# Feature-major input tiles for layer 0, with row factors taken through memory, on one Trainium2 core

## The chip, the cores and the metric

The kernel runs on one core of one Trainium2 chip. The metric is the device time of one execution in microseconds (us). The kernel before was run three times: 3614.48, 3615.36 and 3619.56 us, with a median of 3615.36 us. A separate profiled execution gives the profile and the trace.

The engines are TensorE (PE, with its weight loads shown as PEld), VectorE (DVE), ScalarE (ACT), GpSimd (POOL) and SyncE (SP), which here only issues DMA transfers. ACT and POOL issue transfers too.

## The reference, cut to what matters

The reference is a two-layer backbone over 2304 rows: 256 context rows and 2048 latent rows, 1024 features each. Layer 0 (even) runs latent attention and bidirectional gated linear attention side by side; layer 1 (odd) runs neighbourhood attention. The change touches only how layer 0 makes its normalised and modulated input h, which is the first thing that layer computes:

```
h = rms_norm(x, norm_g[i]) * (1 + scale) + shift      # scale, shift from the conditioning vector
u = h @ w_in                                          # 1056 latent columns first: 768 q, 256 kv, 32 rope
q = rms_norm(q_lat) @ w_uq ; kv = rms_norm(kv_lat) @ w_ukv ; q, k = rms_norm per head, then rope
```

`rms_norm` divides each row by the root of the mean of its squares. So each row of x has one factor, and each feature has one scale and one shift. All arithmetic is in float32. Matmul operands are split in a high and a low part, and each product is three matmuls (high x high, high x low, low x high).

## The kernel before, in words

**Tiles.** The 2304 rows are 18 tiles of 128 rows (`NT`); tiles 0 and 1 are context. A matmul contracts over the partitions, so h must lie with features on the partitions: 8 groups of 128 features (`KD`), each 128 features x 128 rows.

**The stage.** `even_latent` (called once, at the start of the program) holds layer 0's latent projections, up to about 540 us of the span. Tiles 0 and 1 are prepared ahead of its loop. The loop of L584 runs `s` from 0 to 19, and step `s` writes this work:

- `prep(0, s+1)`: makes the input of the next tile. `transposed` (L322) loads 128 rows of `xin` with rows on the partitions (L326, 512 KB, SP), ACT squares them with a running sum for each row (L106, into the tile `hlo`, as a scratch), POOL makes the factor by a power of -1/2 (`rpow`, L204 and L206), DVE scales the rows (L332), and PE transposes the eight 128x128 blocks into the PSUM tiles `px` (L335). `modulate` (L338) then has ACT take each block out of PSUM with the feature's scale and shift (eight instructions, all under L106, the line of the helper `act`), DVE makes the high part (L347, `hhi`) and the low part (L348, `hlo`), and ACT issues the store of h to memory for later stages (L349, `H`).
- `gemm(s)`: three chunks of 352 latent columns, each 24 matmuls of 352 (L120 to L122, PSUM tile `gm`), copied by ACT to `u`, then squares and factors for the latents' norms (`scaled`; DVE scales at L471 and L472).
- `ada`: one or two steps of the conditioning rows for later use. Eight loads of weights (L277, `adaw`, 256 KB each, two buffers), for each two DVE instructions (L280, L282), then two matmuls and a few small instructions (L287 to L311, among them the ones that make `modA` and `modB`, L304 and L306).
- `up(s-1)`: PE transposes the latents (L499, `tp`), ACT and DVE make their high and low parts (`lth`, and `ltl` at L502), 36 matmuls of 384 columns for q and 12 of 512 for k and v (`up`), then norms for each head on ACT, DVE and POOL (L520 to L541).
- `fin(s-2)`: PE transposes q and k for each head (L554), ACT and DVE make high and low parts (`qkhl`, L561), SP stores them (L563). The last tile's keys go through the PSUM tile `px`. In the last steps `first` computes chunks of the next stage for the last two tiles (again `gm` matmuls, now with `W0` to `W2` of that stage).

**What sets the order.** Each engine runs its instructions in the order of its own queue. This order is not the written one: a scheduler that builds the program arranges the instructions of the loop's steps across each other, within the dependences, the number of buffers, and `issue_after`, by which an instruction comes no sooner in the order than another. The conditioning steps are bound to come after the load of x (`self.xload`) in this way. Buffers matter here: `x` has one, `hhi` and `hlo` two each, `adaw` two, `wraw` (raw weights on their way to high and low parts) two, `px`, `tp`, `gm` and `up` two in PSUM.

Of the kernel before, what the change touches and what calls it, by code (L numbers as in the profile page):

```python
# [10 lines left out]
F32 = mybir.dt.float32  # L11
F32R = mybir.dt.float32r
AF = mybir.ActivationFunctionType
ALU = mybir.AluOpType
# [3 lines left out]
P = 128  # L18
D = 1024
KD = D // P  # L20
# [3 lines left out]
NT = T // P  # L24
NCT = CTX // P
EPS = 1e-6
# [19 lines left out]
def win_start(ax, q):  # L46
    n, w, _ = AXES[ax]
    return min(max(q - w // 2, 0), n - w)
# [40 lines left out]
class Kern:  # L89
# [248 lines left out]
    def modulate(self, l, t, x, ps, hi, lo):  # L338
# [10 lines left out]
        nc.scalar.dma_start(self.H[l, t], x[:])  # L349
        return hi, lo  # L350

    def reload(self, l, t):

        nc, sp = self.nc, self.prp
        x = self.tl(sp, [P, D], "x", bufs=1)
        nc.sync.dma_start(x[:], self.H[l, t])
        h = x[:].rearrange("p (k t) -> p k t", k=KD)
        hi = self.tl(sp, [P, KD, P], "hhi", F32R, bufs=self.hbufs)
        lo = self.tl(sp, [P, KD, P], "hlo", F32R, bufs=self.hbufs)
        self.act(hi[:], h)  # L360
        nc.vector.tensor_tensor(out=lo[:], in0=h, in1=hi[:], op=ALU.subtract)
        return hi, lo
# [34 lines left out]
    def even_latent(self, ws, wrest, kept):  # L397
        nc, tc = self.nc, self.tc
        self.QT = self.scr("QT", (A_HEADS, 2, A_QK + 1, T), F32)
        self.KT = self.scr("KT", (A_HEADS, 2, A_QK + 1, T), F32)  # L400
        self.Vn = self.scr("Vn", (P, NT, 512), F32)
        self.Un = self.scr("Un", (NT, P, 1568), F32)
        with ExitStack() as es:
            pp = self.pool(es, "epA", bufs=2, space=PSUM, reuse_waits="tile")
            px = ("px", 2)
            hT, lat, nat, win = {}, {}, {}, {}
            with ExitStack() as es2:
# [4 lines left out]
                hi, lo = win[0] = [self.tl(ws, [P, KD, LAT_CHUNK], "W0" + z, F32R, bufs=1) for z in "hl"]  # L412
# [8 lines left out]
            sp = self.pool(es, "esA", bufs=2, side="left", reuse_waits="tile")  # L421
# [21 lines left out]
            def gemm(*ts):  # L443
                us = {}
                for j in range(3):
                    for t in ts:
                        hi, lo = hT[t]
                        ps = self.tl(pp, [P, LAT_CHUNK], "gm", bufs=2)
                        wh, wl = win[j]
                        self.mm3(ps[:], (lambda k: hi[:, k, :], lambda k: lo[:, k, :]),  # L450
                                 (lambda k: wh[:, k, :], lambda k: wl[:, k, :]), range(KD))
                        if j == 0:
                            us[t] = self.tl(sp, [P, LAT_COLS], "u", bufs=2)
                        self.act(us[t][:, j * LAT_CHUNK : (j + 1) * LAT_CHUNK], ps[:])
                for t in ts:
                    parts = hT.pop(t)
                    if t >= NT - self.hbufs:
                        kept[t] = parts
                    scaled(t, us[t])
# [124 lines left out]
            for s in range(NT + 2):  # L584
                if 0 < s < NT - 1:
                    with tc.issue_after(behind.ins) if s == 1 else ExitStack():
                        hT[s + 1] = self.prep(0, s + 1, self.i["xin"], pp, px)
                if s == 0:
                    gemm(0, 1)
                elif 1 < s < NT:  # L590
                    gemm(s)
                for _ in range((s > 1) + (s in (6, 10))):
                    with tc.issue_after(self.xload.ins):
                        next(ada, None)
                for f, d in ((up, 1), (fin, 2)):
                    if s >= NT - 1:
                        for _ in zip(range(3), ahead):
                            pass
                        if f == fin and s >= NT:
                            first(NT - 1, s - NT + 2)  # L600
                            first(NT - 2, s - NT + 2)
                    if 0 <= s - d < NT:
                        f(s - d)
# [1197 lines left out]
def layout(I):  # L1801

    f = lambda a: np.ascontiguousarray(a, dtype=np.float32)
    o = {}
    o["xin"] = f(np.concatenate([I["ctx"][0], I["x"][0]], 0))
    o["cond"] = f(np.stack([I["c"][0], I["c_ctx"]], -1).reshape(KD, P, 2).transpose(1, 0, 2))
    o["norm_g"] = f(I["norm_g"].reshape(2, KD, P).transpose(2, 0, 1))
    o["ada_w"] = f(I["ada_w"].reshape(2, KD, P, 6, 512).transpose(0, 2, 3, 1, 4))
    o["ada_bc"] = f(I["ada_b"][0, : 2 * D].reshape(2, KD, P).transpose(2, 0, 1))
    o["ada_b"] = f(np.broadcast_to(I["ada_b"][:, None, :], (2, 2, 3 * D)))  # L1810
    w = I["ev_w_in"][0].reshape(KD, P, -1).transpose(1, 0, 2)
    o["w_lat"] = f(w[:, :, :LAT_COLS].reshape(P, KD, 3, LAT_CHUNK).transpose(0, 2, 1, 3))
    o["w_uq"] = f(I["ev_w_uq"][0].reshape(6, P, 768).transpose(1, 0, 2))
    o["w_ukv"] = f(I["ev_w_ukv"][0].reshape(2, P, 1024).transpose(1, 0, 2))
    o["lat_norm"] = f(np.concatenate([I["ev_q_norm"][0].reshape(6, P).T, I["ev_kv_norm"][0].reshape(2, P).T], 1))
    qkg = np.ones((P, 4), np.float32)
    row = np.zeros((2, 32), np.float32)
    for z, g in enumerate((I["ev_q_gain"][0], I["ev_k_gain"][0])):
        qkg[:96, 2 * z] = g
        qkg[:64, 2 * z + 1] = g[:64]  # L1820
        row[z] = g[64:]
    o["qk_gain_col"] = qkg
    o["qk_gain_row"] = row.reshape(1, 2, 32)
    t = np.arange(SEQ)
    inv = np.float32(10000.0) ** (-np.arange(0, 16, 2, dtype=np.float32) / np.float32(16))
    ang = np.stack([(t // 64).astype(np.float32)[:, None] * inv, (t % 64).astype(np.float32)[:, None] * inv], 1)
    cos, sin = np.cos(ang), np.sin(ang)
    C = np.stack([cos, cos], 2).reshape(16, P, 32).transpose(1, 0, 2)
    S = np.stack([-sin, sin], 2).reshape(16, P, 32).transpose(1, 0, 2)
    o["rope_cos"], o["rope_sin"] = f(C), f(S)  # L1830
    r = w[:, :, LAT_COLS:]
    parts = [r[:, :, :512], r[:, :, 1568:], r[:, :, 512:864], r[:, :, 864:1216], r[:, :, 1216:1568]]
    o["w_rest"] = f(np.concatenate([a.reshape(P, -1) for a in parts], 1))
    gw = np.zeros((97, 2, 256), np.float32)
    for z in range(2):
        for r in range(z * 16, 96, 32):
            gw[r : r + 16, z] = I["ev_gate_w"][0, z]
        gw[96, z] = I["ev_gate_b"][0, z]
    o["gate_w"] = f(gw.reshape(97, 2, 4, 64).transpose(0, 2, 1, 3).reshape(97, 512))
    m, l = np.arange(P)[:, None], np.arange(P)[None, :]  # L1840
    tri = np.stack([(m <= l) * 1.0 - (m <= 63), (m >= l) * 1.0 - (m >= 64), m <= l, m >= l], 1)
    o["tri"] = f(tri)
    o["halves"] = f(np.stack([np.arange(P) < 64, np.arange(P) >= 64], 1))
    o["gla_norm"] = f(I["ev_gla_norm"][0].reshape(4, P).T)
    o["w_out0"] = f(I["ev_w_out"][0].reshape(KD, P, D).transpose(1, 0, 2))
    o["w_od"] = f(I["od_w_in"][0].reshape(KD, P, 8, 512).transpose(1, 2, 0, 3))
    o["od_gain"] = f(np.stack([np.tile(I["od_q_gain"][0], 2), np.tile(I["od_k_gain"][0], 2)], 1))
    o["w_out1"] = f(I["od_w_out"][0].reshape(KD, P, D).transpose(1, 0, 2))
    rpb = I["od_rpb"][0]
    for kind in "kq":  # L1850
        off, bad = [], []
        for ax, (_, w, u) in enumerate(AXES):
            start = lambda p: np.array([win_start(ax, x) for x in p.ravel()]).reshape(p.shape)
            at = np.array([p for _, p in BLOCKS[kind][ax]])[None, :]
            own = np.array([g * u for g, _ in BLOCKS[kind][ax]])[None, :] + np.arange(u)[:, None]
            k, q = (own, at) if kind == "k" else (at, own)
            off.append(np.clip(k - q + w - 1, 0, 2 * w - 2))
            bad.append(np.where((k >= start(q)) & (k < start(q) + w), 0, -1e30) * np.ones(off[ax].shape))
        tab = rpb[:, off[0]][..., off[1]]
        if kind == "k":  # L1860
            o["rpb_k"] = f(tab.transpose(0, 3, 1, 2, 4).reshape(16, P, -1))
            rows, cols = np.tile(bad[0], (16, 1)), np.repeat(bad[1], 8, 0)
            o["maskk"] = f(np.minimum(rows[:, :, None], cols[:, None, :]).reshape(P, -1))
        else:
            o["rpb_q"] = f(tab.transpose(0, 1, 3, 2, 4).reshape(16, P, -1))
            rows, cols = np.repeat(bad[0], 16, 0), np.tile(bad[1], (8, 1))
            o["maskq"] = f(np.concatenate([rows, cols], 1))
    return o
# [13 lines left out]
```

## Time and profile before

| | us |
|---|---|
| median of three runs | 3615.36 |
| lowest and highest run | 3614.48, 3619.56 |
| profiled execution | 3617.2 |
| its span, first to last instruction | 3615.4 |
| around the span | 1.8 |
| mean granted TensorE clock | 0.988 of full |

The profile is of one execution. A row of a group of instructions reads: line, engine, operation, output <- inputs, shapes, count, then busy time, the mean of one in ns, and the engine's idle time just before them with what ended it. A row of the timeline reads: start, duration, engine, line, operation, and in brackets idle time before it. A row of waits reads: what waited, for what, then total, number and longest. Matmuls are pipelined, so their durations overlap and their starts tell what one costs. "SPq" and the like are an engine's queue of transfers, whose rows tell when they were issued.

### The profile page before, as it was taken

To read this page: it belongs to the slowest core of one execution; us is meant where nothing else is said; L and a number is where in the kernel's file an instruction comes from. 1 tells how busy PE (TensorE), PEld (TensorE's weight loads), DVE (VectorE), ACT (ScalarE), POOL (GpSimd) and SP (SyncE) were. 2 spreads that over 40 slices of the span, in tenths; PEclk is the share of its full clock that TensorE was granted. 3 is DMA by queue.
4 is the path that set the end of the run, shared out by engine and by line. 5 is a ranking of instruction groups with operands and counts; after the bars stand their busy time and mean duration, and the time that the engine had idled before them with its cause. 6 is when DMAs were issued, how large, how long until landed. Compare 5 with 4: busy or idle time off the path is not lost. (4 is left out here: it accounts for less than half of the span.)

```text
span 3615.4 us, 51630 instructions
## 1 busy us (share of the span) xinstructions
PE 3523.6 (97%) x18260; PEld 2734.3 (76%) x18260; DVE 2372.3 (66%) x4876; ACT 1430.5 (40%) x2705; POOL 1212.6 (34%) x1342
## 2 busy tenths in 40 slices
PE   8999999999999999999999999999999999999899
PEld 6988998888886666656667878888788886555577
DVE  4677665888886776787664345444587874667721
ACT  5544551111115555555653134444422223555510
POOL 1433430111011232212312233333334444677743
PEclk9999999999999999999999999999999999999999
DMA  7555463222233343334534544456643437888654
GB/s 253 149 153 159 141 191 99 87 77 84 75 109 89 83 104 83 94 92 129 163 91 143 162 164 127 145 143 199 212 139 123 139 122 202 213 213 222 185 178 146
DMA packets 396683, 513.62 MB, mean 142 GB/s; under 512 B 61229, under 2 KB 275197, under 8 KB 390522
## 3 DMA queue, kind: packets, MB, share of 16 engines
q1 hardware_dynamic: 353242, 418.68, 40.0%
q0 software_dynamic: 20192, 56.97, 5.6%
q10 hardware_dynamic: 22992, 34.68, 2.8%
q8 instruction: 145, 2.38, 0.3%
q14 instruction: 112, 0.92, 0.1%
HBM read 330.61 MB, written 179.59 MB: 141 GB/s over the span
## 5 line engine op out<-in xcount | busy, mean ns | idle before, releaser
L1007 DVE TENSOR_TENSOR acc<-acc,apt 128x512 f32<-128x512 f32 x512 | 376.4, 764 | 150.6 <-ACT apt L106 147.0
L666 DVE TENSOR_REDUCE mm<-mx 128x1 f32<-128x512 f32 (+1 forms) x656 | 392.7, 627 | 90.6 <-PE mx L665 82.3
L106 ACT ACTIVATE apt<-st 128x512 f32<-128x512 f32 (+1 forms) x592 | 342.9, 593 | 269.0 <-PE st L1018 229.5
L958 PE MATMUL av<-apt,av 128*64 128x512 f32 (+1 forms) x1184 | 269.2, 592 | 0.0
L1016 PE MATMUL st<-aq,akh 97*128 97x512 f32 x576 | 246.8, 428 | 0.2 <-ACT apt L106 0.2
L665 PE MATMUL mx<-mk,mq 96*128 96x512 f32 (+1 forms) x656 | 238.5, 372 | 0.0
L1017 PE MATMUL st<-aq,akh 96*128 96x512 f32 x576 | 229.1, 398 | 0.0
L1018 PE MATMUL st<-aq,akl 96*128 96x512 f32 x576 | 228.5, 397 | 0.0
L1450 DVE CUSTOM_DVE_ANT_1 mx<-mx,mtab 128x465 f32<-128x465 f32 (+14 forms) x576 | 183.9, 338 | 47.2 <-PE mx L1444 34.5
L106 ACT ACTIVATE u<-gm 128x352 f32<-128x352 f32 (+1 forms) x144 | 70.3, 495 | 358.5 <-PE gm L131 207.7
L106 ACT ACTIVATE opt<-opt 128x930 f32<-128x930 f32 (+9 forms) x144 | 119.2, 830 | 234.5 <-POOL opt L1748 137.0
L958 PEld LDWEIGHTS av<-apt,av 128*64 128x64 f32 x1184 | 79.9, 137 | 152.0 <-issue 150.0
L1708 DVE TENSOR_TENSOR opt<-st,tab 128x64 f32<-128x64 f32 (+10 forms) x576 | 143.0, 314 | 78.3 <-PE st L1548 44.7
L1583 POOL TENSOR_TENSOR oacc<-oacc,opt 128x682 f32<-128x682 f32 (+9 forms) x144 | 173.9, 1230 | 37.8 <-ACT opt L106 36.6
L1016 PEld LDWEIGHTS st<-aq,akh 97*128 97x128 f32 x576 | 109.0, 189 | 72.7 <-issue 44.2
L665 PEld LDWEIGHTS mx<-mk,mq 96*128 96x128 f32 x656 | 122.7, 188 | 11.7
L1018 PEld LDWEIGHTS st<-aq,akl 96*128 96x128 f32 x576 | 110.2, 191 | 25.5
L1017 PEld LDWEIGHTS st<-aq,akh 96*128 96x128 f32 x576 | 110.6, 192 | 17.8
L106 ACT ACTIVATE x<-px,modB,modA 128x128 f32<-128x128 f32 x272 | 99.1, 468 | 58.5 <-PE px L335 39.5
L1547 PE MATMUL st<-q,kt 128*128 128x480 f32 (+5 forms) x256 | 98.7, 388 | 20.2 <-DVE opt L1708 14.8
L129 PE MATMUL gm<-w0h,hhi 128*128 128x512 f32 x288 | 115.3, 400 | 2.3 <-DVE hhi L347 2.3
L129 PE MATMUL gm<-w1h,hhi 128*128 128x512 f32 x288 | 116.7, 405 | 0.0
(584 smaller groups left out, 9906.5 us busy)
## 6 DMA issues: line engine op xcount, KB each, us to landing
q<-Q SPq DMA_DIRECT2D x48, 512.0 KB
H<-x ACTq DMA_DIRECT2D x36, 512.0 KB
adaw<-ada_w SPq DMA_DIRECT2D x64, 256.0 KB
x<-H SPq DMA_DIRECT2D x32, 512.0 KB
K1t<-okt POOLq DMA_DIRECT2D x32, 512.0 KB, 6.7
kt<-K1t SPq DMA_DIRECT2D x32, 512.0 KB
mtab<-rpb_q SPq DMA_DIRECT2D x16, 899.0 KB
QT<-qkhl SPq DMA_DIRECT2D x36, 384.0 KB
```

The source lines that it names most:

```text
L106: return self.nc.scalar.activation(out, in_, func, **kw)
L129: self.nc.tensor.matmul(out, lh(k), rh(k), start=j == 0, stop=False)
L665: mm = nc.tensor.matmul(ps[:, :w], q[:A_QK, (t % 6) * P : (t % 6) * P + P], k[:A_QK, k0 : k0 + w], start=True, stop=True)
L666: nc.vector.tensor_reduce(out=m[:, t, n : n + 1], in_=ps[:, :w], axis=AX.X, op=ALU.max)
L958: nc.tensor.matmul(O[j, nb][i * 64 : i * 64 + 64, :w], V[j, kt // TT][:, kt % TT, i * 64 : i * 64 + 64], pts[i][:, :w], start=n == 0, stop ...
L1007: self.add = nc.vector.tensor_tensor(out=acc[i][:, :w], in0=a[:, :w], in1=pts[i][:, :w], op=ALU.add)
L1016: nc.tensor.matmul(ps[:, :w], kh[: A_QK + 1, i, kq], qh[: A_QK + 1, :w], start=True, stop=False)
L1017: nc.tensor.matmul(ps[:, :w], kh[:A_QK, i, kq], ql[:A_QK, :w], start=False, stop=False)
L1018: mm = nc.tensor.matmul(ps[:, :w], kl[:A_QK, i, kq], qh[:A_QK, :w], start=False, stop=True)
L1450: nc.vector.tensor_tensor_reduce(out=s, in0=s, in1=tb[:, ri : ri + rn, ci : ci + cn], scale=1.0, scalar=-3e38, op0=ALU.add, op1=ALU.max, a ...
L1583: self.psum = nc.gpsimd.tensor_tensor(out=a, in0=a, in1=pts[:, :, a0 - r0 : a1 - r0, :], op=ALU.add)
L1708: nc.vector.tensor_tensor(out=pt[:, d[0], d[1]], in0=ps[:, d[0], d[1]], in1=tabs[j][i][:, ri : ri + rn, ci : ci + cn], op=ALU.add)
```

## The change

Memory holds layer 0's input a second time, as `xt`, arranged on the host so that a tile comes with features on the partitions: `xt[t]` is 128 x 8 x 128. Tiles 0 to 3 are made as before. For tiles 4 to 17, `features` loads `xt[t]` into `x` (SP, 512 KB), loads the tile's 128 row factors spread over all partitions (`rb`, 128 x 128, SP, 64 KB written, in the order behind the load of x), has DVE multiply x by them in place, and hands x to `modulate`, which is unchanged: its eight ACT instructions now read and write x in SBUF. These tiles have no transposes and use no `px`.

The factors are made one step earlier by `row_scale`: it loads the rows of `xin` as before (512 KB, now into a `wraw` buffer), squares and sums them on ACT in place, makes the factors on POOL, and stores them (128 x 4 bytes) to `R0` in memory by a transfer that POOL issues.

```
+    def row_scale(self, t):
+        nc, sp = self.nc, self.prp
+        n = self.tl(sp, [P, D], "wraw", bufs=self.wbufs)
+        nc.sync.dma_start(n[:], self.i["xin"][t * P : t * P + P, :])
+        ss = self.tl(sp, [P, 2], "ssx")
+        self.act(n[:], n[:], AF.Square, accum_out=ss[:, 0:1])
+        self.rpow(ss[:, 1:2], ss[:, 0:1], 1.0 / D, EPS)
+        nc.gpsimd.dma_start(self.R0[t].unsqueeze(1), ss[:, 1:2])
+
+    def features(self, t):
+        nc, sp = self.nc, self.prp
+        x = self.tl(sp, [P, D], "x", bufs=1)
+        h = x[:].rearrange("p (k t) -> p k t", k=KD)
+        self.xload = nc.sync.dma_start(h, self.i["xt"][t])
+        hi = self.tl(sp, [P, KD, P], "hhi", F32R, bufs=self.hbufs)
+        lo = self.tl(sp, [P, KD, P], "hlo", F32R, bufs=self.hbufs)
+        rb = self.tl(sp, [P, P], "rb", bufs=1)
+        with self.tc.issue_after(self.xload.ins):
+            nc.sync.dma_start(rb[:], self.R0[t : t + 1].partition_broadcast(P))
+        nc.vector.tensor_tensor(out=h, in0=h, in1=rb[:].unsqueeze(1).to_broadcast([P, KD, P]), op=ALU.mult)
+        return self.modulate(0, t, x, [h[:, :4], h[:, 4:]], hi, lo)
...
+        self.R0 = self.scr("R0", (NT, P), F32)
...
             for s in range(NT + 2):
                 if 0 < s < NT - 1:
                     with tc.issue_after(behind.ins) if s == 1 else ExitStack():
-                        hT[s + 1] = self.prep(0, s + 1, self.i["xin"], pp, px)
+                        hT[s + 1] = self.prep(0, s + 1, self.i["xin"], pp, px) if s <= 2 else self.features(s + 1)
+                        if 2 <= s < NT - 2:
+                            with tc.issue_after(self.xload.ins):
+                                self.row_scale(s + 2)
...
+    o["xt"] = f(o["xin"].reshape(NT, P, KD, P).transpose(0, 3, 2, 1))
```

The changed lines of the kernel after are `row_scale` at L352 to L360 (load L356, store L360) and `features` at L362 to L374 (load of x L367, of factors L372, multiplication L373). Lines behind them move by 24 or 25.

## The prediction

> **What bounds the kernel now.** I read the page's busy shares first, then the busy time of the engines by stretches of the span, then what TensorE (PE) waited for in the stage that the change touches.
>
> ```profile
> span 3615.4 us, 51630 instructions
> PE 3523.6 (97%) x18260; PEld 2734.3 (76%) x18260; DVE 2372.3 (66%) x4876; ACT 1430.5 (40%) x2705; POOL 1212.6 (34%) x1342
> ```
>
> PE is busy 97% of the span. That is an average, so the stage itself has to be looked at. It takes about the first 540 us. The columns are the stretch, its length, then busy time and count of PE, PEld, DVE, ACT and POOL, the granted clock, the DMA share and GB/s.
>
> ```profile
> 100.00:200.00 100.00, 99.11 (x605) 92.31 (x604) 67.11 (x123) 53.19 (x131) 39.85 (x74) 1.00 0.49 142
> 200.00:300.00 100.00, 97.32 (x596) 89.65 (x595) 73.61 (x141) 51.74 (x127) 37.58 (x74) 1.00 0.56 166
> 300.00:400.00 100.00, 96.89 (x571) 87.06 (x570) 72.66 (x141) 48.72 (x118) 42.26 (x76) 0.98 0.50 145
> 400.00:500.00 100.00, 98.95 (x608) 93.45 (x607) 67.61 (x127) 56.12 (x131) 38.32 (x72) 1.00 0.51 148
> ```
>
> From 100 to 500 us PE is busy 97 to 99%, VectorE (DVE) 67 to 74%, ScalarE (ACT) about half, GpSimd (POOL) 40%. PE bounds this stage, and DVE is the nearest of the others. The idle time left on PE between 100 and 470 us, by the instruction that waited and what it waited for:
>
> ```profile
> PE up L122 <- DVE ltl L502: 4.0, 5, 1.8
> PE tp L499 <- DVE modA L306: 2.0, 1, 2.0
> PE tp L554 <- DVE qkhl L561: 0.9, 1, 0.9
> PE tp L499 <- DVE modB L304: 0.4, 1, 0.4
> PE gm L120 <- ACT u L106: 0.3, 1, 0.3
> PE px L335 <- DVE x L332: 0.2, 1, 0.2
> ```
>
> Together 7.8 us. So what leaves PE here leaves the time, except where PE then runs into work that is not ready. Those rows name the work: ltl, modA, qkhl, all made by DVE.
>
> **What the change removes.** For row tiles 4 to 17, 14 tiles, the eight transposes of x on PE (L335). The group of 112 is these 14 tiles; below it are two such blocks with what PE did before and after.
>
> ```profile
> L335 PE MATMUL px<-ident,x 128*128 128x128 f32 x112 | 15.5, 274 | 0.2 <-DVE x L332 0.2
> ```
>
> ```profile
> 114.06 1.03 PE L335 MATMUL px<-ident,x 128*128 128x128 f32 x8
> 114.85 0.41 PE L121 MATMUL gm<-W0l,hhi 128*128 128x352 f32 x1
> ...
> 235.48 0.32 PE L121 MATMUL gm<-W1l,hhi 128*128 128x352 f32 x1
> 235.64 0.60 PE L499 MATMUL tp<-ident,u 128*128 128x128 f32 x4
> 236.07 1.04 PE L335 MATMUL px<-ident,x 128*128 128x128 f32 x8
> 236.87 0.41 PE L122 MATMUL gm<-W1h,hlo 128*128 128x352 f32 x1
> ```
>
> The means overlap, because matmuls are pipelined, so I use starts: from the block's start to the next instruction's start 114.85 - 114.06 = 0.79 us, and 236.87 - 236.07 = 0.80 us. At 0.80 us, 14 blocks are **-11.2 us**. In the same way a gm matmul costs 0.16 us (235.48 to 235.64).
>
> **What it adds on the other engines.** DVE scales x by an operand that is spread over the features, in place of one factor for each row.
>
> ```profile
> L282 DVE SCALAR_TENSOR_TENSOR adac<-adaw,condT,adac 128x512 f32<-128x512 f32 x98 | 69.7, 748 | 10.7 <-DMA adaw<-ada_w 10.4
> L348 DVE TENSOR_TENSOR hlo<-x,hhi 128x512 fp32r<-128x512 f32 x28 | 19.2, 684 | 0.2
> L502 DVE TENSOR_TENSOR ltl<-tp,lth 128x512 fp32r<-128x512 f32 x27 | 18.4, 684 | 7.7 <-ACT lth L106 7.6
> L532 DVE TENSOR_TENSOR qn<-qn,sqk 128x768 f32<-128x768 f32 x14 | 13.4, 954 | 3.2 <-POOL sqk L206 3.0
> L347 DVE CAST hhi<-x 128x512 fp32r<-128x512 f32 x28 | 12.1, 434 | 4.3 <-ACT x L106 4.2
> L332 DVE TENSOR_SCALAR x<-x,ssx 128x1024 f32<-128x1024 f32 x14 | 10.5, 750 | 9.0 <-POOL ssx L206 8.8
> ```
>
> The old scaling is 750 ns (L332). The nearest row with a spread operand is L532, 954 ns for 768 elements, or 1.27 us for 1024. Bounds are 0.75 us (the old form) and 2 x 0.75 = 1.50 us (two L282 of 512). At 1.27 us it is +0.52 us each, 14 x 0.52 = 7.3 us on DVE over some 400 us in which it has about 120 us free. That lies beside PE's work, so I put it at 0; its upper bound, with no cover at all, is 7.3 us.
>
> ACT issues the same instructions: the squares now go over a second copy of the rows, and the eight modulating steps read SBUF in place of PSUM.
>
> ```profile
> L106 ACT ACTIVATE x<-px,modB,modA 128x128 f32<-128x128 f32 x112 | 40.8, 467 | 6.7 <-PE px L335 6.4 <-DMA adaw<-ada_w 0.3
> L106 ACT ACTIVATE sql<-u 128x256 f32<-128x256 f32 x30 | 12.4, 414 | 0.6
> L106 ACT ACTIVATE kn<-up 128x256 f32<-128x256 f32 x28 | 10.8, 384 | 18.1 <-PE up L122 18.1
> ```
>
> SBUF (sql, 414 ns) and PSUM (kn, 384 ns) differ by 30 ns, so 112 steps differ by at most 3.4 us either way, on an engine that is half idle: 0.
>
> POOL gets 14 stores of 128 factors, SP 14 broadcasts of them (64 KB written each) and 14 loads of 512 KB. The nearest store from POOL:
>
> ```profile
> L1465 POOL DMA_DIRECT2D M<-mr x64 | 38.0, 599 | 1.7 <-ACT mr L106 1.3 <-issue 0.4
> ...
> M<-mr POOLq DMA_DIRECT2D x64, 2.0 KB, 1.9
> ```
>
> Issuing takes 0.6 us, 14 x 0.6 = 8.4 us on an engine with 60% free: 0, with 8.4 us as the bound if nothing covered it. The data lands after 1.9 us. The 14 tiles fill 370 us (the group of 112 above), so a tile takes 26 us. Factors are stored one step ahead of the tile that loads them, so the round trip has most of these 26 us.
>
> The Trainium skill, page "SBUF — State Buffer", section "A bandwidth-pool intuition that's wrong (but worth ruling out)", speaks against this part: a DMA issued from GpSimd that takes about 620 ns alone took about 3100 ns beside a VectorE copy, because GpSimd could not write its descriptors. By that rule the stores would cost POOL 14 x 3.1 = 43 us, an estimate, and the sum would still come out the same as long as the tile's step covers it. The 64 stores of M, issued while DVE was at work too, average 599 ns, so this trace does not show it.
>
> On SP the added loads stand ahead of others. In the changed program's order the features' load, the broadcast and the next rows' load come straight ahead of the first weights of a conditioning step (adaw, L277). Before, one load stands there:
>
> ```profile
> 170.52 0.47 SPq L326 DMA_DIRECT2D x<-xin  x1
> 171.04 0.96 SPq L277 DMA_DIRECT2D adaw<-ada_w  x1
> ```
>
> ```profile
> 175.74 1.06 ACT L106 ACTIVATE hlo<-x 128x1024 fp32r<-128x1024 f32 x1 [1.30 <-DMA x<-xin]
> ```
>
> ```profile
> 176.47 0.49 DVE L280 TENSOR_SCALAR adac<-adaw,condT 128x512 f32<-128x512 f32 x1 [3.25 <-DMA adaw<-ada_w]
> ```
>
> x came 175.74 - 170.52 = 5.2 us after its issue, adaw 176.47 - 171.04 = 5.4 us, and DVE stood 3.25 us for it. PE lost nothing there: the waits above hold no such row. Another 576 KB ahead of it takes 0 (another path) to 4.1 us (at the 142 GB/s that the stage moved), and DVE's queue behind it, ltl among it, comes that much later.
>
> **What is late next.** Two places.
>
> First, the middle. The order of the changed program gives most tiles 14 to 23 gm matmuls between the latents' transposes and the matmuls that need ltl: 2.2 to 3.7 us of cover. At three sites there is almost none, and DVE has both casts and both subtractions of the next tile ahead of ltl, which can start only when a gm has freed their buffer: 2 x 0.43 + 2 x 0.68 + 0.68 = 2.9 us. Three such sites are 8.7 us. But the waits of before, 7.8 us, are of the same kind and belong to an order that is gone. So I take the net at **0**, with bounds -7.8 (all old waits go, none come) and +8.7 (all come on top).
>
> Second, the end of the stage. The last tile's keys have to be normalised before PE can transpose them.
>
> ```profile
> 523.50 0.39 PE L122 MATMUL up<-wkvh,ltl 128*128 128x512 f32 x1
> 523.72 0.32 PE L122 MATMUL gm<-W1h,hlo 128*128 128x352 f32 x1
> ...
> 529.90 0.32 PE L122 MATMUL gm<-W1h,hlo 128*128 128x352 f32 x1
> 533.55 1.94 PE L554 MATMUL px<-ident,kn 128*96 128x128 f32 x8 [3.33 <-POOL kn L541]
> ```
>
> From 523.72 to 533.55 us the chain over ACT, DVE and POOL takes 9.8 us. PE fills 6.2 us of it with 34 gm matmuls and 8 transposes of another tile, then waits 3.33 us. The changed order leaves 13 gm matmuls behind the last key matmuls; the other 21 stand ahead of them. The chain is the same, so the wait grows by 21 x 0.16 = **+3.4 us**, to about 6.7 us. After this stage the order of every engine is the old one.
>
> **Sum.** -11.2 + 3.4 + 0 = -7.8 us. The profiled execution took 3617.2 us (span 3615.4 and 1.8 around it), so it would take 3609.4. It lies 1.8 us above the median of the runs, 3615.36, which becomes **3607.6 us**.
>
> **Rivals.**
>
> *More gained.* The old waits go and no new ones come: -11.2 + 3.4 - 7.8 = -15.6, or 3599.8 us; half of them, 3603.7. For it: DVE's scaling no longer stands between POOL's factor and the transposes (8.8 us of DVE idle in L332's row). Against it: the longest of the old waits hang on adaw and ltl, which the change does not touch.
>
> *Given back.* The transposes filled time in which PE would have waited anyway, so that the change doesn't do what it says: the three thin sites cost their 8.7 us on top, -7.8 + 8.7 = +0.9, or 3616.3 us. For it: ltl is already PE's commonest wait. Against it: five waits of at most 1.8 us before, in an order that is no looser.
>
> *Slower.* The first adaw of a conditioning step comes 4.1 us later, behind 576 KB more, DVE stands on it, and ltl behind it in DVE's order is late for PE. With the thinner cover of 2.2 us PE loses 4.1 - 2.2 = 1.9 us a tile, 14 x 1.9 = 26.6 us: 3607.6 + 26.6 = 3634.2 us. The kernel gets slower from 7.8 / 14 = 0.56 us a tile, and by a measurable amount from 15.0 / 14 = 1.1 us. For it: DVE already stood 3.25 us on adaw. Against it: that wait cost PE nothing, and the DMA share is only 0.5.
>
> **How the numbers follow.** 0.2%, about what a measurement of this kernel can tell from no change, is 7.2 us: faster is below 3608.1, slower above 3622.6. The forecast has 0.42; it lies at the edge, and I count 0.24 of it as faster and 0.18 as same. Its own range, with half of the middle's bounds, is 3603.7 to 3612. More gained has 0.24, all faster. Given back has 0.14, all same. Slower has 0.20. Together faster 0.48, same 0.32, slower 0.20. The range starts at 3599, just below the case of more gained, and ends at 3628, inside the slower case, about 0.15 of which lies above.
>
> **What would show it.** L335 with 160 in place of 272 transposes and none of the 14 tiles' px blocks in PE's order; L373 (the new scaling) near 1.27 us; L360 (the store) near 0.6 us; px<-ident,kn waiting about 6.7 us at the stage's end; PE's waits for ltl between 100 and 460 us near 8 us in all. Wrong would be: PE waiting on hhi or hlo (features late), DVE idle for rb or x in L373's row (the round trip is not covered), or DVE idle for adaw well above 10.4 us with PE's wait for ltl grown by as much.

## The result, and the profile after

| | median us | runs | ratio to before, 95% interval |
|---|---|---|---|
| before | 3617.46 | 4 | |
| after | 3701.97 (3700.41 to 3711.01) | 4 | 1.0236 (1.0223 to 1.0249) |

The change makes the kernel 2.4% slower, about 85 us. (The kernel before has one run more here than in the prediction.) The forecast was 3607.6 us, with a range up to 3628.

The page of the kernel after shows as much work as before in a longer span:

```profile
span 3708.6 us, 51486 instructions
PE 3553.4 (96%) x18148; PEld 2754.1 (74%) x18148; DVE 2377.4 (64%) x4876; ACT 1434.7 (39%) x2705; POOL 1245.1 (34%) x1356
```

PE has 112 instructions less, the transposes. The loss must be idle or slow time in the stage, and the same stretches as before show it (stretch, length, busy time and count of PE, PEld, DVE, ACT, POOL, granted clock, DMA share, GB/s):

```profile
100.00:200.00 100.00, 86.56 (x472) 76.64 (x472) 57.49 (x104) 47.50 (x119) 41.04 (x72) 0.93 0.69 148
200.00:300.00 100.00, 86.06 (x468) 77.85 (x467) 62.47 (x115) 40.98 (x98) 41.42 (x65) 0.90 0.65 158
300.00:400.00 100.00, 80.40 (x406) 73.56 (x405) 57.02 (x102) 38.47 (x90) 32.52 (x50) 0.85 0.53 124
400.00:500.00 100.00, 88.00 (x474) 79.87 (x473) 62.91 (x118) 43.97 (x103) 39.95 (x59) 0.90 0.66 155
```

Three things changed together. PE gets through 1820 matmuls in these 400 us, where it did 2380, and it is idle for 59.0 us of them, where it was for 7.7 us. Its granted clock falls to 0.85 to 0.93. And the DMA engines are busier (0.53 to 0.69, before 0.49 to 0.56) while they move no more bytes each second. The last point is the odd one: busy engines that carry no more.

What PE waited for from 60 us to the end of the stage:

```profile
PE up L122 <- DVE ltl L527: 17.3, 6, 6.7
PE up L120 <- ACT lth L106: 8.5, 5, 3.5
PE tp L579 <- DVE qkhl L586: 8.2, 5, 4.4
PE tp L287 <- DVE qkhl L586: 8.2, 2, 5.2
PE px L579 <- POOL kn L566: 6.7, 1, 6.7
```

The last row is the stall at the end of the stage, 3.3 us before and forecast at 6.7. The others are new or grown. Behind them stand DVE's waits (first row; the kernel before has 11.3 us in the same stretch) and ACT's (second):

```profile
DVE adac L282 <- DMA adaw<-ada_w: 62.0, 31, 7.6
```

```profile
ACT wraw L106 <- DMA wraw<-xin: 47.6, 9, 8.1
```

Both wait for transfers. One tile shows how a transfer comes to be late. First POOL's store of the factors, then the broadcast load, which SP can issue when the store has landed:

```profile
113.43 0.63 POOL L360 DMA_DIRECT2D R<-ssx  x1 [0.30 <-POOL ssx L206]
```

```profile
114.13 0.44 SPq L356 DMA_DIRECT2D wraw<-xin  x1
...
121.54 0.34 SPq L372 DMA_DIRECT2D rb<-R  x1
```

The store is issued at 113.43 us and has landed by 121.54. SP stands still for it, and the weights (`adaw`) behind the broadcast load with it. That part holds for this tile alone: over the whole execution SP waits for a store once, and issues the other 13 broadcast loads without a wait for one.

```profile
SPq L372 <- DMA R<-ssx: 5.8, 1, 5.8
```

What holds up the transfers that are already under way is another thing. The DMA engines while the store is in flight, and after it:

```profile
117.00:122.00 5.00, 5.00 (x36) 4.96 (x35) 2.58 (x6) 0.40 (x1) 3.13 (x5) 1.00 0.91 48
124.00:126.00 2.00, 0.00 (x0) 0.00 (x0) 0.00 (x0) 0.73 (x1) 0.00 (x0) 1.00 1.09 352
```

From 117 to 122 us the engines are 0.91 busy and move 48 GB/s; from 124 to 126 us they are as busy and move 352 GB/s. Transfers that have nothing to do with the factors nearly stand still for some 5 us. The load of the next rows, issued at 114.13, is one of them. ACT, DVE and PE follow, in this order:

```profile
125.27 1.06 ACT L106 ACTIVATE wraw<-wraw 128x1024 f32<-128x1024 f32 x1 [7.87 <-DMA wraw<-xin]
```

```profile
127.16 0.75 DVE L586 SCALAR_TENSOR_TENSOR qkhl<-tp,qkg,qkhl 96x512 fp32r<-96x512 f32 x1 [6.84 <-ACT qkhl L106]
```

```profile
127.96 3.43 PE L287 MATMUL tp<-adac,pick 128*2 128x512 f32 x4 [5.19 <-DVE qkhl L586]
```

ACT stands 7.87 us at the squares, with qkhl queued behind them; DVE stands 6.84 us for qkhl; PE's next matmul wants the PSUM tile that qkhl is read from, and stands 5.19 us. Then the clock:

```profile
128.00:131.00 3.00, 3.00 (x4) 0.30 (x4) 2.92 (x4) 1.89 (x6) 2.97 (x4) 0.50 0.87 270
132.00:135.00 3.00, 3.00 (x20) 3.00 (x20) 2.45 (x5) 2.31 (x7) 0.00 (x0) 1.00 0.68 183
```

When PE works again, its granted clock is 0.50 for the 3 us from 128 to 131, which is up to 1.5 us lost on top of the wait of 5.19. The Trainium skill, page "TensorE: Matmul & The Clock Gate", section "Part 1: The HAM clock gate (the "warmup" mystery)", says that an idle window of about 3.4 us brings the half-rate clock. This wait agrees, but the traces show that a shorter one is enough. In the kernel before no wait of PE between 100 and 470 us is longer than 2.0 us, and behind one of these the clock is 0.50 as well:

```profile
345.80:349.20 3.40, 1.45 (x11) 1.10 (x9) 3.40 (x7) 1.05 (x2) 0.00 (x0) 1.00 0.60 207
349.20:352.60 3.40, 3.14 (x12) 2.85 (x11) 3.25 (x6) 0.86 (x3) 0.00 (x0) 0.50 0.66 204
```

Over 100 to 500 us the granted clock averages 0.895 (the four rows above; 0.995 before), so up to 0.10 x 400 = 40 us of the loss is slow clock, an upper bound, because some of it falls on idle time. The added idle time is 59.0 - 7.7 = 51.3 us. Together they are enough for the 85 us.

All 14 stores land late, 7.4 to 10.2 us after their issue (the row has 13 of them: count, KB, median us from issue to landing), though POOL issues them in 0.65 us:

```profile
R<-ssx POOLq DMA_DIRECT2D x13, 0.5 KB, 8.1
```

```profile
L360 POOL DMA_DIRECT2D R<-ssx x13 | 8.4, 647 | 3.3 <-POOL ssx L206 3.3
L373 DVE TENSOR_TENSOR x<-x,rb 128x1024 f32<-128x1024 f32 x14 | 17.5, 1248 | 11.9 <-DMA rb<-R 10.1 <-issue 1.7
```

The theory was then: the stores, 128 pieces of 4 bytes side by side, hold up every transfer. Rival 1: the added loads (512 KB and 64 KB a tile), or the broadcast. Rival 2: the new order of the instructions.

### The profile page after: what moved, and what is told of

Its sections match the earlier page's. It is cut to its first block, busy times and chain, and to the rows that moved or that the text cites. A ratio compares the mean times of both kernels' runs of the same rounds, so it can differ in the third digit from the quotient of the medians.

```text
span 3708.6 us, 51486 instructions
## 1 busy us (share of the span) xinstructions
PE 3553.4 (96%) x18148; PEld 2754.1 (74%) x18148; DVE 2377.4 (64%) x4876; ACT 1434.7 (39%) x2705; POOL 1245.1 (34%) x1356
## 3 DMA queue, kind: packets, MB, share of 16 engines
q0 software_dynamic: 20640, 56.98, 5.4%
## 4 chain that ended last, share of the span: by engine, by line
PE 70%; issue 11%; DMA 7%; DVE 6%; POOL 3%; ACT 2%; SPq 0%; POOLq 0%; DVEq 0%; ACTq 0%
PE gm L131 7%; PE gm L129 7%; PE gm L130 7%; PE av L986 7%; PE st L1044 4%; PE st L1045 3%; PE st L1046 3%; DMA adaw<-ada_w 3%; PE st L1575 2%; PE o L1605 2%; PE st L129 2%; PE st L131 2%; PE st L130 2%; PE o L1587 2%; PE st L1576 1%
## 5 line engine op out<-in xcount | busy, mean ns | idle before, releaser
L282 DVE SCALAR_TENSOR_TENSOR adac<-adaw,condT,adac 128x512 f32<-128x512 f32 x112 | 80.1, 746 | 62.4 <-DMA adaw<-ada_w 62.0
```

## The experiments

Each ratio is to runs of the kernel before on the same chip. "Cover" is the number of gm matmuls that stand in PE's order between the latents' first transposes of a tile and the first up matmul that needs them; a tile is called thin below 5. This is counted from the programs' orders, for tiles 4 to 16. The kernel before has two thin tiles (7, 10), and the changed kernel has six in its trace (5 to 10), three of them with no gm matmul at all.

### Stores or loads

e1_no_store takes the store out and loads 128 other numbers, from the input rows, so it leaves out the right scaling:

```
-        nc.gpsimd.dma_start(self.R0[t].unsqueeze(1), ss[:, 1:2])
+        self.fac = ss
...
-            nc.sync.dma_start(rb[:], self.R0[t : t + 1].partition_broadcast(P))
+            nc.sync.dma_start(rb[:], self.i["xin"][t : t + 1, :P].partition_broadcast(P))
```

> The changed kernel without the 14 stores of the factors; the broadcast load takes 128 numbers of the tile's input row instead, so the rows are scaled by wrong numbers and the factors are left unused. All loads, the broadcast and the order of the steps stay. Theory (the stores clog every transfer for some 8 us each, the landing time of L360): about 3617.5 - 7.8 = 3610 us, DVE's idle time for adaw back near 10 us, PE's wait for kn at the stage's end near 6.7 us. Rival 1 (576 KB more of loads ahead of adaw, or the broadcast itself): stays at 3690 to 3705 us, with DVE idle some 60 us for adaw. Rival 2 (the new order with thin cover): stays at 3690 to 3705 us as well, with PE's waits for ltl, lth and qkhl as in the changed kernel.

Measured: 3653.11 us, ratio 1.0093 (1.0074 to 1.0111). DVE's waits for adaw in e1_no_store, between 60 and 600 us:

```profile
DVE adac L282 <- DMA adaw<-ada_w: 21.3, 31, 2.1
```

They fall from 62.0 to 21.3 us with every load still there, so rival 1 isn't the larger part of adaw's delay; up to 10 us of it may be the loads' (before: 11.3). But the time is neither 3610 nor 3700: the store is a part, and something else keeps some 34 us.

e2_store_alone adds the store to the kernel before and nothing else; the scheduler's order comes out somewhat different by it:

```
+        nc.gpsimd.dma_start(self.R0[t].unsqueeze(1), ss[:, 1:2]) if src is self.i["xin"] and t > 3 else None
```

> The kernel before, plus only the 14 stores of the factors of tiles 4 to 17 by POOL; nothing reads them, and transposes and loads are those of before. Theory (the stores clog the transfers): well slower, 3640 to 3710 us, with each store landing after some 8 us and DVE's idle time for adaw well above 10 us. Both rivals (load volume; new order): 3617 to 3622 us, since 14 x 0.64 us on POOL is hidden.

Measured: 3666.05 us, 1.0128 (1.0104 to 1.0152), or 46 us for 14 stores that nobody reads. Whether it is the stores or the new order, e3_store_apart below will tell. Their landing in e2_store_alone:

```profile
R<-ssx POOLq DMA_DIRECT2D x14, 0.5 KB, 8.6
```

e4_act_store leaves the changed kernel as it is and issues the store from ACT:

```
-        nc.gpsimd.dma_start(self.R0[t].unsqueeze(1), ss[:, 1:2])
+        nc.scalar.dma_start(self.R0[t].unsqueeze(1), ss[:, 1:2])
```

> The changed kernel with the factors' store issued by ACT's queue in place of POOL's; the computation is complete. If the 4-byte pieces clog the transfers whoever issues them: 3680 to 3710 us, about as the changed kernel. If it is POOL's software queue that clogs them: 3608 to 3616 us. Rivals (load volume; order): 3690 to 3705 us.

Measured: 3719.40 us, 1.0275 (1.0245 to 1.0305), above the range that was expected. The store costs no less from ACT's queue, so POOL's queue isn't the cause.

### What it is in the store

e3_store_apart and e15_store_64 are e2_store_alone with the same 4-byte pieces 512 and 64 bytes apart. In the traces of the three, PE, DVE, ACT and POOL run the same instructions in the same order:

```
-self.R0 = self.scr("R0", (NT, P), F32)
+self.R0 = self.scr("R0", (NT, P, P), F32)      # e15_store_64: (NT, P, 16)
...
-nc.gpsimd.dma_start(self.R0[t].unsqueeze(1), ss[:, 1:2])
+nc.gpsimd.dma_start(self.R0[t, :, 0:1], ss[:, 1:2])
```

> The kernel before plus the 14 stores alone, as in e2_store_alone (3666 us), with the same order of instructions, but each factor's 4 bytes go to a place 512 bytes from the next. Nothing reads them. If 128 pieces of 4 bytes side by side clog the transfers because they fall on the same stretch of memory: 3616 to 3624 us and a landing time near 2 us. If any piece of 4 bytes does: 3655 to 3675 us and a landing time near 8 us. Theories that blame order or loads expect no difference to e2_store_alone.

> As e2_store_alone (3666 us) and e3_store_apart (3619 us), in the same order, with the 4-byte pieces 64 bytes apart. If only pieces in the same 64 bytes get in each other's way: 3616 to 3624 us and a landing time near 2 us. If pieces within the same 512 bytes do: between the two, 3625 to 3660 us, with a landing time between 2 and 8 us.

Measured: 3619.38 us, 0.9998 (0.9987 to 1.0008), for 512 bytes, and 3622.75 us, 1.0004 (0.9992 to 1.0015), for 64. Both cost nothing. Their landing, e3_store_apart first:

```profile
R<-ssx POOLq DMA_DIRECT2D x14, 0.5 KB, 2.1
```

```profile
R<-ssx POOLq DMA_DIRECT2D x14, 0.5 KB, 2.1
```

DVE's waits for adaw between 60 and 600 us, in e2_store_alone and in e3_store_apart:

```profile
DVE adac L282 <- DMA adaw<-ada_w: 46.3, 20, 7.1
```

```profile
DVE adac L282 <- DMA adaw<-ada_w: 9.4, 16, 1.4
```

This shows the first of the two causes, since the order is the same. The software queue, which holds POOL's transfers, has 20640 packets in each of the three kernels and 20192 before: 448 more, or 32 for each of the 14 stores. So neither the number of the pieces, nor their size, nor the number of packets does it, but how near they lie in memory: 2.1 us at a distance of 64 or 512 bytes, 8.6 us at 4 bytes. The Trainium skill, page "DMA: Bandwidth & Descriptors", section "Specifications", says that transfers under 512 bytes are read, modified and written back; these pieces are all under 512 bytes, so by that rule alone the three kernels would be alike, and the runs show that they aren't. That pieces which fall on the same stretch wait for one another would fit, but is only argued.

### The rest of the loss

e6_pe_factors makes the broadcast on PE, with no way through memory:

```
-        nc.gpsimd.dma_start(self.R0[t].unsqueeze(1), ss[:, 1:2])
+        self.fac[t] = ss
...
+        rb = self.tl(pp, [P, 4, P], px[0], bufs=px[1])[:, 0, :]
+        nc.tensor.transpose(rb, self.fac.pop(t)[:, 1:2].to_broadcast([P, P]), self.ident[:])
+        nc.vector.tensor_tensor(out=h, in0=h, in1=rb.unsqueeze(1).to_broadcast([P, KD, P]), op=ALU.mult)
```

> The changed kernel with no way through memory for the factors: PE transposes the column of 128 factors, read 128 times over, into a PSUM tile (one transpose of 128 a tile), and DVE multiplies by it from there. The second load of the rows and the squares stay; the computation is complete. Theory (the stores did it): 3617.5 - 7.8 + 14 x 0.1 = about 3611 us. Rival 1 (load volume, 512 KB more a tile): 3690 us or more. Rival 2 (order): 3680 us or more.

Measured: 3643.93 us, 1.0065 (1.0041 to 1.0089). The theory of the stores alone falls here; it explains the larger part (58 of the 85 us go with them), not the whole. Some waits of PE in e6_pe_factors, 60 to 600 us, and two stretches:

```profile
PE px L371 <- POOL ssx L206: 5.5, 5, 2.6
PE up L122 <- DVE ltl L526: 5.0, 3, 3.6
PE tp L523 <- DVE modB L304: 4.7, 2, 2.6
PE up L120 <- ACT lth L106: 3.9, 4, 1.5
PE tp L301 <- DVE adab L296: 3.7, 4, 1.2
```

```profile
200.00:300.00 100.00, 89.73 (x506) 81.35 (x507) 70.73 (x135) 48.10 (x115) 45.21 (x68) 0.93 0.57 171
300.00:400.00 100.00, 89.93 (x493) 81.88 (x493) 67.21 (x126) 46.90 (x112) 36.94 (x64) 0.91 0.52 154
```

The first row belongs to the new small transposes (L371). Apart from the stall for kn at the stage's end (7.3 us) no wait is over 3.8 us, and none is for a transfer. The two stretches hold tiles 5 to 10 or so, and of these five are thin in its order (5, 7, 8, 9, 10); the kernel before has two (7, 10).

e8_no_rows takes the second load, the squares and the powers out of e6_pe_factors:

```
-        n = self.tl(sp, [P, D], "wraw", bufs=self.wbufs)
-        nc.sync.dma_start(n[:], self.i["xin"][t * P : t * P + P, :])
-        ss = self.tl(sp, [P, 2], "ssx")
-        self.act(n[:], n[:], AF.Square, accum_out=ss[:, 0:1])
-        self.rpow(ss[:, 1:2], ss[:, 0:1], 1.0 / D, EPS)
+        ss = self.mhalf
```

> e6_pe_factors (3644 us) without the second load of the rows, their squares and powers: the transposed column is a constant, so the rows are not scaled by their own factors. If the remaining loss is the second load (SP's and ACT's wait for it, 31 us of ACT idle for wraw): 3606 to 3614 us. If it is the order, which leaves the latents' transposes without cover ahead of the up matmuls for six tiles between 200 and 370 us: 3630 to 3645 us.

Measured: 3641.81 us, 1.0055 (1.0035 to 1.0075), level with e6_pe_factors: the second load isn't it.

e9_cover and b9_cover force the order, by issue_after: the latents' transposes (`head`) ahead of the next tile's second gm chunk, the rest of `up` (`tail`) behind it, on e6_pe_factors and on the kernel before:

```
+                        with tc.issue_after(mid().ins) if mid and j == 1 else ExitStack():
+                            self.mm3(ps[:], (lambda k: hi[:, k, :], lambda k: lo[:, k, :]),
+                                     (lambda k: wh[:, k, :], lambda k: wl[:, k, :]), range(KD))
+                        self.cover[j] = self.lastmm
...
+                    with tc.issue_after(self.cover[1].ins):
+                        tail(t)
...
+                    gemm(s, mid=(lambda: head(s - 1)) if s > 3 else None)
```

> e6_pe_factors with the order forced: the latents' transposes of a tile come ahead of the second chunk of the next tile's gm matmuls, and the up matmuls behind that chunk, so that 48 gm matmuls (7.7 us) stand between. The computation is complete. If the remaining loss is the thin cover in the order: 3600 to 3614 us, TensorE waits between 100 and 500 us below 10 us and granted clock 1.00 in 200 to 400 us. If it is the second load or the features' chain: 3630 to 3645 us.

> The kernel before with the same forced order (48 gm matmuls between the latents' transposes and the up matmuls of each tile), the eight transposes of x kept. Its 7.8 us of TensorE waits between 100 and 470 us can go: 3608 to 3618 us. e9_cover against it is the price of the transposes: about 11 us less 14 x 0.1 and less what else differs, so e9_cover should be 6 to 11 us faster than this one if the removed transposes are a gain in a covered order.

Measured: 3701.73 us, 1.0219 (1.0204 to 1.0234), and 3680.77 us, 1.0162 (1.0145 to 1.0179). Both expectations missed widely. The waits moved, here in e9_cover:

```profile
PE tp L527 <- DVE qkhl L602: 51.5, 25, 5.6
```

The latents' transposes now stood for the PSUM tile tp, which the heads' transposes still held. So a large cover isn't enough, and tp is where the three users meet: latents, heads, conditioning steps. This pointed to px, which the change leaves nearly unused.

b10_no_transposes takes nothing but the transposes out of the kernel before, so h lies the wrong way round in it; in `transposed`, ahead of the PSUM tiles:

```
+        if t > 3 and xp is None and src is self.i["xin"]:
+            h = x[:].rearrange("p (k t) -> p k t", k=KD)
+            return x, [h[:, :4], h[:, 4:]], hi, lo
```

> The kernel before without the eight transposes of x for tiles 4 to 17 and with nothing in their place: ACT reads the rows as if they were features, so h is wrong for these tiles. No second load, no factors through memory, no new multiplication. In its order five tiles (5, 6, 7, 9, 10) are without cover, two more or three than before. If the removed PE time is a plain gain: 3617 - 11.2 + 3 = 3606 to 3611 us. If the scheduler's new order gives it back by thin cover: 3620 to 3645 us, with TensorE waiting for lth, ltl and qkhl between 200 and 370 us and the clock granted below 0.95 there.

Measured: 3636.62 us, 1.0038 (1.0023 to 1.0053). Taking 112 matmuls from the engine that bounds the stage, and adding nothing, makes the kernel slower. Five tiles are thin. Its waits, 60 us to the end of the stage:

```profile
PE px L557 <- POOL kn L544: 7.6, 1, 7.6
PE up L122 <- DVE ltl L505: 7.2, 5, 2.8
PE up L120 <- ACT lth L106: 5.9, 7, 2.5
PE tp L301 <- DVE adab L296: 4.3, 2, 2.2
PE tp L502 <- DVE modB L304: 4.2, 1, 4.2
```

Then one edit of the PSUM tile, on e6_pe_factors (e12_up_px), on the kernel before (b12_up_px), on b10_no_transposes (b14_no_tr_up_px) and on the changed kernel (a12_up_px):

```
-                    ps = self.tl(pp, [P, 4, P], "px" if t == NT - 1 else "tp")
+                    ps = self.tl(pp, [P, 4, P], "px")
```

> e6_pe_factors (3644 us) with one edit: the latents' transposes of every tile go to the PSUM tile px, which the change has left nearly unused, in place of tp, which they share with the conditioning steps and the heads' transposes. In its order 10 to 24 gm matmuls stand between the latents' first transposes and the up matmuls of every tile from 4 to 16 (e6_pe_factors: none or nearly none for five tiles). If the thin cover is what cost the rest: 3600 to 3612 us, faster than before, and granted clock 1.00 from 200 to 400 us. If it is the features' chain or the loads: 3630 to 3645 us.

> The kernel before with the px edit alone (the latents' transposes in px, shared with the transposes of x). Its order leaves 13 to 24 gm matmuls of cover for every tile from 3 to 16. If e12_up_px is faster because of the removed transposes: 3614 to 3620 us, and e12_up_px faster than this by 4 to 10 us. If the px edit alone is the gain: 3604 to 3611 us, level with e12_up_px.

> b10_no_transposes (3637 us) with the px edit; h is wrong for tiles 4 to 17, as there. Every tile from 3 to 16 has 14 to 22 gm matmuls of cover. If thin cover gave the removal back: 3603 to 3611 us, about 11 us below b12_up_px less what the end of the stage takes (3 us). If it is something else in the removal: 3625 us or more.

> The changed kernel itself, stores and loads of the factors through memory included, with the px edit. If the two causes add up: 3609 + 35 to 55 us for the stores = 3645 to 3665 us, DVE idle 40 us or more for adaw. If the cover hides the stores' hold-ups: 3610 to 3630 us.

| | us | ratio, 95% interval | thin tiles |
|---|---|---|---|
| b12_up_px | 3619.21 | 0.9996 (0.9986 to 1.0006) | 0 |
| e12_up_px | 3609.40 | 0.9965 (0.9955 to 0.9976) | 0 |
| b14_no_tr_up_px | 3603.71 | 0.9945 (0.9925 to 0.9964) | 0 |
| a12_up_px | 3689.27 | 1.0186 (1.0160 to 1.0212) | 0 |

e12_up_px beats both kernels, the one before by 0.35%. The px edit alone does nothing (b12_up_px), so the gain needs the removed transposes; and the removed transposes alone lose (b10_no_transposes), so they need the px edit. PE's waits of e12_up_px between 100 and 470 us:

```profile
PE tp L301 <- DVE adab L296: 2.9, 2, 1.9
PE gm L120 <- ACT u L106: 2.4, 3, 1.3
PE gm L122 <- DVE hlo L348: 1.8, 1, 1.8
```

None for ltl, lth or qkhl is left. DVE still waits 21.2 us for adaw between 60 and 600 us, as in e1_no_store, so that much costs nothing here. In b14_no_tr_up_px the stretch from 200 to 300 us is full at full clock:

```profile
200.00:300.00 100.00, 99.68 (x600) 92.01 (x599) 75.58 (x146) 54.56 (x132) 43.91 (x81) 1.00 0.55 161
```

With the stores and the broadcast loads put back (a12_up_px), 80 us come back with them, more than the 35 to 55 expected. SP waits for a store only once here too, for 1.0 us. Its landing time, and the time DVE stands for adaw from 100 to 500 us:

```profile
R<-ssx POOLq DMA_DIRECT2D x13, 0.5 KB, 9.5
```

```profile
  DMA adaw<-ada_w: 50.0, 16
```

Two more moved the order about: e11_ada_px on e6_pe_factors (first edit), e13_all_thin on e12_up_px (second, the call of `features` moved behind `up`).

```
-... for b in range(6)], sp, pp, "tp")
+... for b in range(6)], sp, pp, "px")
...
+                    if f == up and 2 < s < NT - 1:
+                        hT[s + 1] = self.features(s + 1, pp, px)
```

> e6_pe_factors with the conditioning steps' PSUM tiles moved from tp to px in place of the latents' transposes. Two tiles are left without cover (8 and 12). If thin cover is what costs, at about 9 us a thin tile: 3615 to 3630 us, between e12_up_px and e6_pe_factors. If not: 3640 to 3650 us.

> e12_up_px with the features' call written behind up in each step: the same instructions, and an order that leaves no gm matmul between the latents' first transposes and the up matmuls for nearly all tiles from 5 to 16. If thin cover is what costs: some 12 thin tiles at about 9 us each above e12_up_px, 3690 to 3740 us. If the order of these matmuls does not matter: as e12_up_px within 10 us.

e11_ada_px took 3623.06 us, 1.0016 (1.0003 to 1.0028), as expected with two thin tiles. e13_all_thin took 3647.53 us, 1.0070 (1.0049 to 1.0091): eleven thin tiles, slower than e12_up_px by 38 us, but far from the 80 to 130 expected. So thin tiles go with loss, and there is no fixed price for one: some 3.5 us here, and at most (3643.93 - 3609.40) / 5 = 6.9 us between e6_pe_factors and e12_up_px, whose only edit is the PSUM tile.

## Why the prediction was wrong, step by step

- **The transposes, -11.2 us: right in size, where nothing else gives way.** e12_up_px against b12_up_px is 3609.40 - 3619.21 = -9.8 us, with 14 small transposes and the loads in it, on two chips on which the kernel before took 3620.30 and 3620.42 us. b14_no_tr_up_px, which adds nothing, is 15.5 us below b12_up_px; its four runs spread over 13 us, so this doesn't part -11.2 from the -15.6 of the rival that gains more.
- **The stores at 0, bound 8.4 us: this step failed, and it is most of the loss.** The step priced what the store costs POOL, and this held (0.65 us, forecast 0.6). It took the landing time from the nearest row, 1.9 us for a store of 2 KB, and asked only whether the round trip fits into a tile's 26 us, which it does. It didn't ask what the transfer does to the others. The row was far in just the respect that counts: the pieces of this store are 4 bytes, side by side. Measured: 8.1 us to land, and 47 us in one order of instructions (e2_store_alone against e3_store_apart), 80 us in a covered order, broadcast loads included (a12_up_px against e12_up_px).
- **The middle at 0, between -7.8 and +8.7: failed as well.** Three thin sites were seen and priced at 2.9 us each, and set off against the old waits; the changed kernel's trace has six, three with no gm matmul and three with 2 or 3. b10_no_transposes shows that the removal alone, with its new order, costs 0.38% (14 us) where -7.8 was summed; e6_pe_factors 0.65% (24 us). The price missed the PSUM tile that the latents' transposes share, and the lower clock behind the waits: 0.93 and 0.91 in e6_pe_factors from 200 to 400 us, where before had 1.00 and 0.98.
- **The end of the stage, +3.4 us: right as a wait.** kn: 6.7 us, forecast about 6.7. No run shows what it costs by itself: e3_store_apart waits 5.8 us there and is level with the kernel before.
- **DVE's multiplication: right.** 1.25 us (forecast 1.27), beside other work. Its waits for rb, 10.1 us, were the sign named for a round trip that isn't covered, but the sign misleads: SP waited for a store only once, and e1_no_store, which has no round trip, waits 9.0 us for rb.
- **The slower rival (0.20) had the place and not the reason.** It had adaw late, DVE standing on it, and PE's wait for ltl grown: 62.0 and 17.3 us. It put that down to 576 KB more ahead of adaw, at 1.9 us a tile. e1_no_store keeps these loads and has 21.3. And its price, 26.6 us, was a third of the loss.
- **Given back (0.14)** is what b10_no_transposes does, though by more than its +0.9 us.

What stays open: the px edit changes both the sharing of PSUM and the order that follows from it, and no run parts the two. e1_no_store and e6_pe_factors differ by 9 us (1.0093 and 1.0065), with intervals that touch, and e1_no_store has one thin tile more in its trace (six, 5 to 10), so the broadcast load may cost a little or nothing. The cause behind the distance of the pieces in memory is open as well. Distances between 4 and 64 bytes were not tried.

## What to carry to other kernels

When a step sends something small through memory, look at how its pieces lie there, and judge it by the landing time and by what every other transfer does meanwhile, not by the issuing engine's time alone. When work leaves the engine that bounds a stage, the order is made anew: look for which shared buffer and which chain now stands bare, and give the freed buffer to it. Count the clock beside the waits: here 51 us more of idle time on PE came with up to 40 us of slow clock.

## What was not expected of the hardware

- One store of 512 bytes in 128 pieces of 4 bytes side by side lands after 8.1 to 9.5 us (medians of three kernels) and holds up unrelated transfers on the way (48 GB/s from 117 to 122 us, with the engines 0.91 busy); the same pieces 64 or 512 bytes apart land after 2.1 us and cost nothing. Issued from ACT the store is no better (3719 us).
- After a wait of 5.19 us on PE the granted clock was 0.50 from 128 to 131 us. In the kernel before, it was 0.50 from 349.2 to 352.6 us, behind a wait of only 2.0 us; PE had been busy for 1.45 of the 3.40 us ahead of it.
- PE can transpose a column that is read 128 times over: 14 of these in e12_up_px take the place of 112 transposes and of the way through memory.
